# Heads of 64 features: high and low parts stacked, two products for each score and value product

## The chip, the cores and the metric

The kernel runs on one core of one Trainium2 chip. The metric is the device time of one launch in microseconds, as the median of three runs. TensorE multiplies matrices into PSUM banks of 128 x 512 numbers; VectorE, ScalarE and GpSimd work on tiles of 128 partitions; SyncE issues the DMA transfers of the weights.

## The reference

A sequence of 512 tokens with 1024 features goes through two layers of a first block (hybrid mixer, cross attention to a memory, convolutional feed-forward) and two layers of a second block. The change lies in two of the sublayers.

The mixer of the first block has two attention branches with 8 query heads and 2 key heads of 64 features each. Branch a looks at a band of 128 positions to either side, with a learned sink; branch b looks at all positions:

```
s = einsum('bnqkgd,bnskd->bnkgqs', qb, kw) / sqrt(64);  s = where(valid, s, -inf)      # branch a
p = softmax(concat([s, sink]))[..., :-1];  o = einsum('bnkgqs,bnskd->bnqkgd', p, vw)
s = einsum('bqkgd,bskd->bkgqs', qblk, k) / sqrt(64);  p = softmax(s);  o = einsum('bkgqs,bskd->bqkgd', p, v)   # branch b
```

A third branch is a gated product over positions. Each branch goes through its own weights, times a sigmoid gate of the input, and the sum through one more product. The first layer of the second block has an indexer: 16 query heads of 64 features against one key, `relu(q k)` weighted and summed over heads, of which the 256 largest per query choose the keys of another attention.

## The kernel before, in words

All products are made to float32 precision from float32r pieces: every operand is split in a high part (a rounded copy, by ScalarE) and a low part (what is left, by VectorE), and `mm3` (lines 129 to 133) issues three products for each: high by high, high by low, low by high. They run over weight units of 128 x 1024 numbers, brought by DMA and split by `W` (lines 146 and 150).

For 64 features `heads_ab` makes the queries of 4 head pairs c and the keys, turns them by TensorE transposes into feature-major tiles of 128 partitions (`to_fm`, L611), in which one head takes partitions 0 to 63 and the other 64 to 127, and splits them. A score product then contracts over 64 partitions, `r = slice(64 * half, 64 * half + 64)`. Scores of one head and one tile of 128 queries go to one of two PSUM banks (tile `pss`); a maximum (L797 in branch b, L759 with the mask in a), an exp with its sum (L800, L763) and a scaling by the reciprocal (L805, L772) make the four tiles of P, which lie in the tiles `v` for the first head of a pair and `w` for the second. `pt_av` (from L656) transposes P (L665, tile `pt`, two banks), splits it (L166 and L167, tile `t`), and multiplies by the values. The values of a pair lie side by side with 64 zero columns between them, so that both heads, one after the other, add into the two halves of one PSUM bank (tile `po`, there is one), which is split at the end of the pair. The indexer does its scores likewise in `score`, with one bank more, and ScalarE's relu frees the bank.

The program's order is not that of the code: a scheduler sets each engine's queue from its own estimate of the times, and where an attention chain has to wait, TensorE gets products of what comes next in the code. These are the products of the tile `mm`: the projections of the next branch, the gates and the branch weights (`branch`). `branch` of the gated part follows branch a, that of a and of b follow branch b, and the last needs the result of b. Three banks hold `mm` tiles, so the products of branch b's weights can't run far ahead of its attention.

Of the kernel before, what the change touches and what calls it, by code (L numbers as in the profile page):

```python
# [49 lines left out]
class Kernel:  # L50
# [65 lines left out]
    @contextmanager  # L116
    def behind(self, *marks):
        """what is issued inside follows the marked instructions on their engines."""
        with ExitStack() as es:
            for m in marks:  # L120
                es.enter_context(self.tc.issue_after(m))
            yield

    def mark(self):
        """the last instruction issued."""
        return self.nc.cur_bb.bb.instructions[-1]

# [7 lines left out]
    def W(self, ap, kc, tag=None):  # L135
        """weight unit [128, kc*w] in high and low parts; returns block k -> (high, low) [128, w]."""
# [22 lines left out]
    def split(self, role, src, n=512, scale=None):  # L159
        """src (PSUM or SBUF, f32), by row times scale -> (high, low) f32r tiles."""  # L160
# [9 lines left out]
    def lin(self, units, kc, xs, post, n=512, head=0, tail=0, mid=None, tags=(), spare=False, late=None):  # L170
        """feature-major product; unit = [128, kc*w], w/128 output chunks of kc blocks. The first head chunks
        take the two token halves one after the other; the last tail chunks do so as a group, with mid between.
        tags: where the last units' weights go; spare: two score banks are free after the head.
        late: (n, marks): the weights from unit n on are taken behind the marks."""
# [60 lines left out]
    def tok(self, units, xs, post, tiles=4, w=256):  # L235
        """token-major product; units split the contraction; psum pair tiles [128, 2, w]."""
# [13 lines left out]
    def tok_head(self, items, xs):  # L250
        """the first products (blocks, post, w) together, token half by token half; token-major, but the first."""
# [29 lines left out]
    def rstd(self, v, n):  # L281
        """v ** -0.5 on a small tile: a few by power on GpSimd and one Newton step, more from the exponent's half
        by Newton's iteration."""
# [35 lines left out]
    def sq_add(self, st, src, c, first=False):  # L319
        """src ** 2 joins the sum of squares (first: begins it for tokens c)."""  # L320
# [24 lines left out]
    def ln_chunk(self, st, xs, m, c):  # L345
        """centred chunk m joins the sums of values and squares."""
# [9 lines left out]
    def ln_pilot(self, st, x, c):  # L356
        """the mean of the first chunk, about which all statistics are taken."""
# [7 lines left out]
    def ln_stats(self, st, c, eps):  # L365
        """-> PSUM bank with 1/std and mean/std of the 256 tokens c, on all partitions."""
# [21 lines left out]
    def pipe(self, n, stages, strict=True):  # L388
        """stages of one instruction each over n items, in step: on every engine the oldest item first."""
# [8 lines left out]
    def ln_apply(self, bc, xs, g, b, c, post, own=2):  # L398
        """normalises the 256 tokens c; every own-th mean off on GpSimd (own 1: every second gain there too);
        post: what follows, a function of k per instruction."""  # L400
# [31 lines left out]
    def xsplit(self, out, src, c):  # L432
        """high and low parts of src(k) [128, tokens c] into the k-th pair of out, in two steps."""
# [33 lines left out]
    def last(self, units, kc, xs, resid, norm, tail=4, head=0, tags=(), sums=1, late=None):  # L467
        """a sublayer's last product, its norm following by token halves: norm(half) yields after the
        statistics of each stage; the first half's sums are taken behind sums chunks more of the tail."""
# [37 lines left out]
    def resid_ln(self, st):  # L507
        """adds a product to the scaled residual, centres it and takes the statistics."""
# [23 lines left out]
    def resid_part(self, st, part):  # L532
        """the same for a product in three parts: centred about the pilot of the first two."""
# [19 lines left out]
    def norm_ln(self, st, g, b, out, nxt=None):  # L553
        """post-norm by token halves into out; nxt = gain of a second (RMS) norm on top."""
# [52 lines left out]
    def to_fm(self, role, srcs, ps=None, scale=None):  # L607
        """four token-major [128, 128] pieces -> feature-major [128, 512] (high, low)."""
# [5 lines left out]

    def rope(self, src, out, tab, p, nh, dh, blocks, half):
        """src, out [128, 2, nh*dh]; tab [128, 512] = cos | signed sin, each [4 tiles, dh];
        rotates blocks of 2*half within each head of dh."""
# [19 lines left out]
    def rope_part(self, x, tab, p, nh, dh, rot):  # L637
        """in place on the first rot dims of each head of x [128, 2, nh*dh]; tab [128, 2*4*rot]."""
# [17 lines left out]
    def pt_av(self, out, pap, nkt, qr, vap, first=True, last=True, keep=None):  # L656
        """out += v^T P^T over the key tiles; pap(qt, kt) = P piece, vap(kt) = (high, low)."""
        nc = self.nc
        for kt in range(nkt):
# [11 lines left out]
            vh, vl = vap(kt)  # L671
            self.mm3(out[:, q0 * 128:q1 * 128], vh, vl, h[:, :n], l[:, :n], first and kt == 0, last and kt == nkt - 1)

# [4 lines left out]
    def heads_ab(self, l, br, xs, tabs, mid=None):  # L678
        """projections of an attention branch: q (4 head pairs) and k feature-major, v token-major; mid runs
        after the first."""  # L680
# [56 lines left out]

    def attn_a(self, qkv, sink):
        nc = self.nc
        Q, (kh, kl), V, _ = qkv  # L740
        nsink = self.sm(8)
        nc.vector.tensor_scalar(nsink, sink, -1.0, None, op0=ALU.mult)
        out = []
# [1048 lines left out]
```

## Time and profile before

| | |
|---|---|
| runs | 3522.07 us median (3520.36 to 3522.11) |
| profiled execution, span from first to last instruction | 3519.9 us |
| TensorE products | 19440, busy 98% of the span |
| VectorE, ScalarE, GpSimd | busy 60%, 43%, 11% |
| granted TensorE clock, mean | 0.991 of full speed |

A profiled execution gives its span; its own time on the device's clock isn't told, and the timed runs lie 0.5 to 2.2 us above the span. A product is shown from its issue to its modelled end, so products overlap: the distance of their starts says what one costs, not its duration. Lines are those of the kernel before.

### The profile page before, as it was taken

The numbers are of one execution on the slowest core, as the hardware profiler recorded it, in microseconds if no ns is written. First come the engines' busy times: TensorE is split into PE (matmuls) and PEld (weight loads), VectorE is DVE, ScalarE is ACT, GpSimd is POOL, SyncE is SP. The second block draws the span as 40 slices with busy tenths as digits, with TensorE's granted clock in tenths as the row PEclk, the third lists the DMA queues.
The fourth block names the chain that finished last, engine by engine and source line by source line (L and its number), as shares of the span: only waits on it lengthen the run. The fifth ranks groups of instructions, "written<-read, shape, count | busy, mean of one in ns | idle before, by whom it ended". The sixth has DMA issues, their size and how long they took to land.

```text
span 3519.9 us, 49472 instructions
## 1 busy us (share of the span) xinstructions
PE 3442.7 (98%) x19440; PEld 2977.4 (85%) x19440; DVE 2122.4 (60%) x3874; ACT 1498.4 (43%) x2786; POOL 385.1 (11%) x588
## 2 busy tenths in 40 slices
PE   9999999999999999999999998999999998999999
PEld 8897798888898877988888788889888887988887
DVE  5576587655665765775557578565333698664333
ACT  3444355433434444553334446353222576442222
POOL 0000012000000000120001243000000286110000
PEclk9999999999999999999999998999999999999999
DMA  4221231333322212313333122222333322223333
GB/s 143 72 64 58 63 124 60 96 98 96 97 90 68 72 49 80 113 61 108 96 96 88 48 81 83 78 91 83 96 97 95 101 73 84 78 67 92 100 96 96
DMA packets 87929, 302.40 MB, mean 86 GB/s; under 512 B 10000, under 2 KB 10768, under 8 KB 87696
## 3 DMA queue, kind: packets, MB, share of 16 engines
q1 hardware_dynamic: 87696, 299.24, 27.9%
q8 instruction: 153, 2.51, 0.3%
q14 instruction: 80, 0.66, 0.1%
HBM read 297.10 MB, written 2.10 MB: 85 GB/s over the span
## 4 chain that ended last, share of the span: by engine, by line
PE 75%; issue 12%; DVE 7%; POOL 2%; ACT 2%; DMA 2%; DVEq 0%; POOLq 0%; ACTq 0%
PE mm L131 20%; PE mm L132 20%; PE mm L133 20%; PE pss L131 2%; PE pss L133 2%; PE pss L132 2%; PE pt L665 2%; PE mm L195 1%; PE po L132 1%; PE po L131 1%; PE po L133 1%; DVE wl L150 1%; PE po L195 1%; DVE pss L1414 1%; PE mm L198 1%
## 5 line engine op out<-in xcount | busy, mean ns | idle before, releaser
L146 ACT CAST wh<-wraw 128x1024 fp32r<-128x1024 f32 (+2 forms) x496 | 514.0, 1039 | 953.3 <-PE mm L132 475.5
L150 DVE TENSOR_TENSOR wl<-wraw,wh 128x1024 fp32r<-128x1024 f32 (+2 forms) x487 | 599.2, 1232 | 509.8 <-ACT wh L146 504.1
L131 PE MATMUL mm<-xh,wh 128*128 128x512 f32 (+1 forms) x2152 | 821.5, 382 | 8.2 <-ACT xh L437 6.0
L132 PE MATMUL mm<-xl,wh 128*128 128x512 f32 (+1 forms) x2152 | 822.8, 382 | 1.2 <-DVE xl L440 1.1
L133 PE MATMUL mm<-xh,wl 128*128 128x512 f32 (+1 forms) x2152 | 820.8, 381 | 0.0
L131 PEld LDWEIGHTS mm<-xh,wh 128*128 128x128 f32 x2152 | 405.5, 189 | 86.6 <-ACT xh L437 6.4
L132 PEld LDWEIGHTS mm<-xl,wh 128*128 128x128 f32 x2152 | 405.6, 188 | 82.4 <-issue 5.5
L133 PEld LDWEIGHTS mm<-xh,wl 128*128 128x128 f32 x2152 | 405.5, 188 | 80.1 <-issue 5.6
L131 PE MATMUL mm<-wh,xh 128*128 128x256 f32 x768 | 220.2, 287 | 0.0
L133 PE MATMUL mm<-wh,xl 128*128 128x256 f32 x768 | 219.1, 285 | 0.0
L132 PE MATMUL mm<-wl,xh 128*128 128x256 f32 x768 | 219.0, 285 | 0.0
L131 PE MATMUL mm<-p,wh 128*128 128x512 f32 (+1 forms) x556 | 202.1, 371 | 6.3 <-DVE x L524 4.3
L133 PE MATMUL mm<-p,wl 128*128 128x512 f32 (+1 forms) x556 | 205.1, 369 | 0.0
L132 PE MATMUL mm<-p,wh 128*128 128x512 f32 (+1 forms) x556 | 204.0, 367 | 0.0
L376 POOL TENSOR_TENSOR s<-s 128x2 f32<-128x2 f32 x14 | 7.0, 502 | 1576.8 <-ACT s L373 1576.8
L131 PE MATMUL mm<-o,wh 128*128 128x512 f32 (+1 forms) x456 | 170.2, 373 | 0.0
L132 PE MATMUL mm<-o,wh 128*128 128x512 f32 (+1 forms) x456 | 169.4, 371 | 0.0
L133 PE MATMUL mm<-o,wl 128*128 128x512 f32 (+1 forms) x456 | 169.2, 371 | 0.0
L1123 DVE TENSOR_TENSOR x<-x,mm 128x512 f32<-128x512 f32 (+1 forms) x102 | 57.0, 565 | 164.7 <-PE mm L133 164.6
L131 PEld LDWEIGHTS mm<-wh,xh 128*128 128x128 f32 x768 | 146.8, 191 | 4.6 <-issue 3.9
L133 PEld LDWEIGHTS mm<-wh,xl 128*128 128x128 f32 x768 | 146.9, 191 | 4.2 <-issue 3.9
L132 PEld LDWEIGHTS mm<-wl,xh 128*128 128x128 f32 x768 | 146.9, 191 | 3.5 <-issue 2.6
(636 smaller groups left out, 7166.8 us busy)
## 6 DMA issues: line engine op xcount, KB each, us to landing
wraw<-fup SPq DMA_DIRECT2D x88, 512.0 KB, 3.5
wraw<-gup SPq DMA_DIRECT2D x88, 512.0 KB, 3.6
wraw<-wg SPq DMA_DIRECT2D x48, 512.0 KB, 3.5
wraw<-wt SPq DMA_DIRECT2D x32, 512.0 KB, 3.5
wraw<-fdn SPq DMA_DIRECT2D x32, 512.0 KB, 3.5
wraw<-gdn SPq DMA_DIRECT2D x32, 512.0 KB, 3.5
wraw<-wbr SPq DMA_DIRECT2D x24, 512.0 KB, 3.5
wraw<-wab SPq DMA_DIRECT2D x20, 512.0 KB, 3.5
```

Of the source, the lines that this page charges most:

```text
L131: mm(out, lh, rh, start=first, stop=False, skip_group_check=True)
L132: mm(out, lh, rl, start=False, stop=False, skip_group_check=True)
L133: mm(out, ll, rh, start=False, stop=last, skip_group_check=True)
L146: nc.scalar.copy(h[i][:, :e], raw[:, i * e:(i + 1) * e])
L150: eng.tensor_tensor(l[i][:, :e], raw[:, i * e:(i + 1) * e], h[i][:, :e], op=ALU.subtract)
L195: self.nc.tensor.matmul(out, w[:, c], xs[k][0][:, t], start=first and k == 0 and w is h, stop=False, skip_group_check=True)
L198: self.nc.tensor.matmul(out, h[:, c], xs[k][1][:, t], start=False, stop=k == kc - 1, skip_group_check=True)
L376: g.tensor_tensor(t, m, m, op=ALU.mult)
L665: nc.tensor.transpose(ps[:, i * 128:(i + 1) * 128], pap(qt, kt), self.ident)
L1123: self.nc.vector.tensor_add(x, x, ps)
L1414: nc.vector.scalar_tensor_tensor(acc[:, s:], a[:, :S - s], w(s), acc[:, s:], op0=ALU.mult, op1=ALU.add)
```

## The change

`to_stack` replaces `to_fm` for queries of 64 features. For each head of a pair it makes a tile of its own, with the head's high part on one half of the partitions and its low part on the other, by a copy of 64 partitions and a subtraction of 64 partitions, whose result goes to the other half. `to_twice` writes the keys of each key head twice, on both halves, as a high and a low tile. Two products over 128 partitions (`mm2`) then hold all four terms: stacked query by high key, stacked query by low key. The values get their low columns where the zeros were: a tile of 128 columns holds a head's high and low part. Two products with the high and low part of P give the two halves in the two halves of the partitions of a PSUM bank, and `join` adds them: a ScalarE copy of 64 partitions to the place of the head, and a VectorE addition. The bank `po` is thus taken and freed once a head, not once a pair; the split follows from SBUF. The indexer's queries are stacked in the same way; its key was on both halves before. Attention with 128 features keeps `mm3`.

```diff
+    def to_stack(self, role, srcs):
+        nc = self.nc
+        ps = self.pst()
+        for i, a in enumerate(srcs):
+            nc.tensor.transpose(ps[:, i * 128:(i + 1) * 128], a, self.ident)
+        out = []
+        for r, q in ((slice(0, 64), slice(64, 128)), (slice(64, 128), slice(0, 64))):
+            t = self.T(role, F32R)
+            nc.scalar.copy(t[r], ps[r])
+            nc.vector.tensor_sub(t[q], ps[r], t[r])
+            out.append(t)
+        return out
+    def to_twice(self, role, srcs):
+        nc = self.nc
+        ps = self.pst()
+        for i, a in enumerate(srcs):
+            nc.tensor.transpose(ps[:, i * 128:(i + 1) * 128], a, self.ident)
+        out = []
+        halves = slice(0, 64), slice(64, 128)
+        for r in halves:
+            h, l = self.T(role, F32R), self.T(role, F32R)
+            for q in halves:
+                nc.scalar.copy(h[q], ps[r])
+                nc.vector.tensor_sub(l[q], ps[r], h[q])
+            out.append((h, l))
+        return out
+    def mm2(self, out, q, kh, kl):
+        mm = self.nc.tensor.matmul
+        mm(out, q, kh, start=True, stop=False, skip_group_check=True)
+        mm(out, q, kl, start=False, stop=True, skip_group_check=True)
...
-            vh, vl = vap(kt)
-            self.mm3(out[:, q0 * 128:q1 * 128], vh, vl, h[:, :n], l[:, :n], first and kt == 0, last and kt == nkt - 1)
+            v, o = vap(kt), out[:, q0 * 128:q1 * 128]
+            if isinstance(v, tuple):
+                self.mm3(o, *v, h[:, :n], l[:, :n], first and kt == 0, last and kt == nkt - 1)
+                continue
+            nc.tensor.matmul(o, v, h[:, :n], start=first and kt == 0, stop=False, skip_group_check=True)
+            nc.tensor.matmul(o, v, l[:, :n], start=False, stop=last and kt == nkt - 1, skip_group_check=True)
+    def join(self, out, o, half):
+        r, q = (slice(64 * i, 64 * i + 64) for i in (half, 1 - half))
+        self.nc.scalar.copy(out[r], o[q])
+        self.nc.vector.tensor_add(out[r], out[r], o[r])
...
-            vh, vl = self.T("r", F32R, [128, 2, 3, 64]), self.T("r", F32R, [128, 2, 3, 64])
-            z = self.ident.rearrange("p (t c) -> p t c", t=2)
-            nc.vector.tensor_scalar(vh[:, :, 1], z, 0.0, None, op0=ALU.mult)
-            nc.vector.tensor_scalar(vl[:, :, 1], z, 0.0, None, op0=ALU.mult)
+            v = self.T("r", F32R, [128, 2, 4, 64])
             src = ps[:, :, 128:256].rearrange("p t (h c) -> p t h c", h=2)
-            nc.scalar.copy(vh[:, :, 0::2], src)
-            nc.vector.tensor_sub(vl[:, :, 0::2], src, vh[:, :, 0::2])
-            V[p] = (vh.rearrange("p t a c -> p t (a c)"), vl.rearrange("p t a c -> p t (a c)"))
+            nc.scalar.copy(v[:, :, 0::3], src)
+            nc.vector.tensor_sub(v[:, :, 1:3], src, v[:, :, 0::3])
+            V[p] = v.rearrange("p t a c -> p t (a c)")
...
-        Q = [self.to_fm("q", [qt[c // 2, t // 2][:, t % 2, (c % 2) * 128:(c % 2 + 1) * 128] for t in range(4)]) for c in range(4)]
-        Kt = self.to_fm("r", [kt[t // 2][:, t % 2, :] for t in range(4)])
+        Q = [self.to_stack("q", [qt[c // 2, t // 2][:, t % 2, (c % 2) * 128:(c % 2 + 1) * 128] for t in range(4)]) for c in range(4)]
+        Kt = self.to_twice("r", [kt[t // 2][:, t % 2, :] for t in range(4)])
...
     def attn_b(self, qkv):
         nc = self.nc
-        Q, (kh, kl), V, rq = qkv
+        Q, Kt, V, rq = qkv
         out = []
         for c in range(4):
-            o = self.po()
+            both = self.T("w")
             for half in range(2):
-                r = slice(64 * half, 64 * half + 64)
+                o = self.po()
+                kh, kl = Kt[half]
                 P = []
                 nm, sm = self.sm(4), self.sm(4)
                 for qt in range(4):
                     ps = self.pss()
-                    self.mm3(ps, Q[c][0][r, qt * 128:(qt + 1) * 128], Q[c][1][r, qt * 128:(qt + 1) * 128],
-                             kh[r, :], kl[r, :], True, True)
+                    self.mm2(ps, Q[c][half][:, qt * 128:(qt + 1) * 128], kh, kl)
                     i = ((c // 2) * 2 + qt // 2) * 8 + (qt % 2) * 4 + (c % 2) * 2 + half
                     nc.vector.tensor_reduce(nm[:, qt:qt + 1], ps, axis=AX.X, op=ALU.max, negate=True)
                     nc.vector.tensor_tensor(nm[:, qt:qt + 1], nm[:, qt:qt + 1], rq[:, i:i + 1], op=ALU.mult)
...
                 nc.vector.reciprocal(sm, sm)
                 for qt in range(4):
                     nc.vector.tensor_scalar(P[qt], P[qt], sm[:, qt:qt + 1], None, op0=ALU.mult)
-                vap = lambda kt: tuple(a[:, kt % 2, 64 * half:64 * half + 128] for a in V[kt // 2])
-                self.pt_av(o, lambda qt, kt: P[qt][:, kt * 128:(kt + 1) * 128], 4, lambda kt: (0, 4), vap,
-                           half == 0, half == 1)
-            out.append(self.split("p", o))
+                vap = lambda kt: V[kt // 2][:, kt % 2, 128 * half:128 * half + 128]
+                self.pt_av(o, lambda qt, kt: P[qt][:, kt * 128:(kt + 1) * 128], 4, lambda kt: (0, 4), vap)
+                self.join(both, o, half)
+            out.append(self.split("p", both))
...
-            r = slice(64 * (h % 2), 64 * (h % 2) + 64)
             s = slice(qt * 128, (qt + 1) * 128)
             ps = self.po() if qt == 2 else self.pss()
-            self.mm3(ps[:, :n], Q[0][r, s], Q[1][r, s], ikh[r, :n], ikl[r, :n], True, True)
+            self.mm2(ps[:, :n], Q[h % 2][:, s], ikh[:, :n], ikl[:, :n])
...
-                Q = self.to_fm("op"[u // 2], [it[u][t // 2][:, t % 2, c * 128:(c + 1) * 128] for t in range(4)])
+                Q = self.to_stack("op"[u // 2], [it[u][t // 2][:, t % 2, c * 128:(c + 1) * 128] for t in range(4)])
```

`attn_a` is changed as `attn_b`. The scheduler then sets another order. On TensorE, in branch b of the first layer, in the last head pair (P in `w` is of the pair's second head, P in `v` of the first; `pss` are scores, `pt` transposes, `po` value products, `mm` products of other work), before:

```order
L132 MATMUL po<-t,r 128x512
L133 MATMUL po<-t,r 128x512
L665 MATMUL pt<-ident,w 128x128 x6
L131 MATMUL pss<-r,q 128x512
L132 MATMUL pss<-r,q 128x512
L133 MATMUL pss<-r,q 128x512
L131 MATMUL pss<-r,q 128x512
L132 MATMUL pss<-r,q 128x512
L133 MATMUL pss<-r,q 128x512
L132 MATMUL mm<-xl,wh 128x512
L133 MATMUL mm<-xh,wl 128x512
L131 MATMUL mm<-o,wh 128x512
```

And now, at the same place (the last `v` tiles are that pair's first head):

```order
L714 MATMUL po<-t,r 128x512
L703 MATMUL pt<-ident,v 128x128 x4
L713 MATMUL po<-t,r 128x512
L714 MATMUL po<-t,r 128x512
L713 MATMUL po<-t,r 128x512
L714 MATMUL po<-t,r 128x512
L649 MATMUL pss<-r,q 128x512
L650 MATMUL pss<-r,q 128x512
L649 MATMUL pss<-r,q 128x512
L650 MATMUL pss<-r,q 128x512
L703 MATMUL pt<-ident,w 128x128 x8
L713 MATMUL po<-t,r 128x512
```

Before, twelve and more `mm` products follow a group of scores; now the scores of the next tiles, the transposes and the value products stand next to one another.

On ScalarE at this place (`t` is a part of P transposed, `p` a part of the result, `wh` a weight's high part, `f` a gate), before:

```order
L800 ACTIVATE v,s<-pss,s 128x512 x2
L166 CAST t<-pt 128x512 x2
L800 ACTIVATE v,s<-pss,s 128x512 x2
L146 CAST wh<-wraw 128x1024
L883 ACTIVATE f<-mm,pv 128x512
L166 CAST t<-pt 128x512 x2
L800 ACTIVATE w,s<-pss,s 128x512 x2
L166 CAST p<-po 128x512
L166 CAST t<-pt 128x512 x2
```

And now:

```order
L719 COPY w<-po 64x512
L166 CAST t<-pt 128x512
L166 CAST p<-w 128x512
L166 CAST t<-pt 128x512 x3
L719 COPY w<-po 64x512
L847 ACTIVATE w,s<-pss,s 128x512 x4
L166 CAST t<-pt 128x512
L847 ACTIVATE v,s<-pss,s 128x512 x2
L166 CAST t<-pt 128x512 x2
L847 ACTIVATE v,s<-pss,s 128x512 x2
```

Copies of the join (`w<-po`) stand ahead of the exps of the next head (L847) and of the cast of the pair's result (`p<-w`), once a head; weight casts and gates are gone from the stretch.

## Rows read from the trace of the kernel before

**Rows 1.** the page: busy shares of engines, then the chain that ended last

```profile
PE 3442.7 (98%) x19440; PEld 2977.4 (85%) x19440; DVE 2122.4 (60%) x3874; ACT 1498.4 (43%) x2786; POOL 385.1 (11%) x588
...
PE 75%; issue 12%; DVE 7%; POOL 2%; ACT 2%; DMA 2%; DVEq 0%; POOLq 0%; ACTq 0%
```

**Rows 2.** stretches: length, then PE, PEld, DVE, ACT, POOL busy, clock, DMA

```profile
181.00:250.00 69.00, 69.00 (x488) 63.58 (x487) 51.41 (x150) 29.85 (x67) 0.00 (x0) 1.00 0.20 62
...
310.00:360.00 50.00, 50.00 (x235) 38.57 (x233) 34.26 (x67) 23.99 (x46) 0.00 (x0) 1.00 0.18 53
1990.00:2060.00 70.00, 70.00 (x433) 55.03 (x432) 39.66 (x58) 35.94 (x88) 14.87 (x22) 1.00 0.15 46
```

**Rows 3.** TensorE's timeline in branch b: start, duration, instruction

```profile
370.41 0.40 PE L132 MATMUL mm<-xl,wh 128*128 128x512 f32 x1
370.74 0.49 PE L131 MATMUL pss<-r,q 64*128 64x512 f32 x1
371.07 0.39 PE L132 MATMUL pss<-r,q 64*128 64x512 f32 x1
371.31 0.39 PE L133 MATMUL pss<-r,q 64*128 64x512 f32 x1
371.63 0.50 PE L133 MATMUL mm<-xh,wl 128*128 128x512 f32 x1
371.96 0.40 PE L131 MATMUL mm<-xh,wh 128*128 128x512 f32 x1
372.20 0.39 PE L132 MATMUL mm<-xl,wh 128*128 128x512 f32 x1
372.43 0.40 PE L133 MATMUL mm<-xh,wl 128*128 128x512 f32 x1
```

**Rows 4.** lines by form, branch b: count, busy us, mean ns, idle before

```profile
L797 DVE TENSOR_REDUCE s<-pss 128x1 f32<-128x512 f32 x32 | 21.8, 687 | 4.7 <-PE pss L133 4.5
L167 DVE TENSOR_TENSOR t<-pt,t 128x512 fp32r<-128x512 f32 x30 | 20.4, 685 | 16.5 <-ACT t L166 16.5
...
L805 DVE TENSOR_SCALAR w<-w,s 128x512 f32<-128x512 f32 x16 | 6.7, 482 | 0.1
...
L798 DVE TENSOR_TENSOR s<-s 128x1 f32<-128x1 f32 x32 | 4.6, 154 | 0.2
...
L166 ACT CAST t<-pt 128x512 fp32r<-128x512 f32 x31 | 17.1, 590 | 20.6 <-PE pt L665 20.6
...
L800 ACT ACTIVATE v<-pss,s 128x512 f32<-128x512 f32 x16 | 12.4, 777 | 20.7 <-DVE s L798 20.7
...
L800 ACT ACTIVATION_READ_ACCUMULATOR w<-pss,s 128x1 f32 x16 | 3.1, 194 | 0.0
```

**Rows 5.** timeline of branch b's last transposes and its end

```profile
396.22 0.60 PE L665 MATMUL pt<-ident,w 128*128 128x128 f32 x4
396.57 0.48 PE L132 MATMUL po<-t,r 128*128 128x512 f32 x1
...
403.33 0.51 PE L131 MATMUL mm<-p,wh 128*128 128x512 f32 x1 [0.68 <-ACT p L166]
```

**Rows 6.** lines by form of VectorE, branch a

```profile
L167 DVE TENSOR_TENSOR t<-pt,t 128x384 fp32r<-128x384 f32 x16 | 8.9, 554 | 6.2 <-ACT t L166 6.2
L167 DVE TENSOR_TENSOR t<-pt,t 128x256 fp32r<-128x256 f32 x16 | 6.7, 420 | 3.8 <-ACT t L166 3.7
L761 DVE TENSOR_SCALAR s<-s 128x1 f32<-128x1 f32 x32 | 6.0, 208 | 0.1
...
L759 DVE CUSTOM_DVE_ANT_0 w<-pss,mask 128x384 f32<-128x384 f32 x8 | 4.4, 552 | 0.8 <-PE pss L133 0.7
...
L772 DVE TENSOR_SCALAR w<-w,s 128x384 f32<-128x384 f32 x8 | 3.0, 415 | 0.0
```

**Rows 7.** a stretch of few products: busy times and clock

```profile
2150.00:2160.00 10.00, 7.21 (x18) 3.88 (x19) 6.58 (x11) 8.16 (x17) 2.78 (x8) 0.52 0.38 122
```

**Rows 8.** TensorE's timeline in that stretch

```profile
2155.68 0.80 PE L131 MATMUL mm<-v,wh 128*128 128x512 f32 x1 [0.55 <-ACT v L166]
```

More of the change, by code (lines that the diff above doesn't have):

```diff
@@ L739, in attn_a @@
         nc = self.nc
-        Q, (kh, kl), V, _ = qkv
+        Q, Kt, V, _ = qkv
         nsink = self.sm(8)
@@ L754, in attn_a @@
                     ps = self.pss()
-                    self.mm3(ps[:, :n], Q[c][0][r, qt * 128:(qt + 1) * 128], Q[c][1][r, qt * 128:(qt + 1) * 128],
-                             kh[r, k0 * 128:k1 * 128], kl[r, k0 * 128:k1 * 128], True, True)
+                    self.mm2(ps[:, :n], Q[c][half][:, qt * 128:(qt + 1) * 128], kh[:, k0 * 128:k1 * 128],
+                             kl[:, k0 * 128:k1 * 128])
                     pt = self.T("vw"[half])
@@ L776, in pap @@
                     return P[qt][:, o0:o0 + 128]
-                vap = lambda kt: tuple(a[:, kt % 2, 64 * half:64 * half + 128] for a in V[kt // 2])
-                self.pt_av(o, pap, 4, lambda kt: (max(0, kt - 1), min(4, kt + 2)), vap, half == 0, half == 1)
-            out.append(self.split("o", o))
+                vap = lambda kt: V[kt // 2][:, kt % 2, 128 * half:128 * half + 128]
+                self.pt_av(o, pap, 4, lambda kt: (max(0, kt - 1), min(4, kt + 2)), vap)
+                self.join(both, o, half)
+            out.append(self.split("o", both))
         return out
@@ L783, in attn_b @@
         nc = self.nc
-        Q, (kh, kl), V, rq = qkv
+        Q, Kt, V, rq = qkv
         out = []
         for c in range(4):
-            o = self.po()
+            both = self.T("w")
             for half in range(2):
-                r = slice(64 * half, 64 * half + 64)
+                o = self.po()
+                kh, kl = Kt[half]
                 P = []
@@ L805, in attn_b @@
                     nc.vector.tensor_scalar(P[qt], P[qt], sm[:, qt:qt + 1], None, op0=ALU.mult)
-                vap = lambda kt: tuple(a[:, kt % 2, 64 * half:64 * half + 128] for a in V[kt // 2])
-                self.pt_av(o, lambda qt, kt: P[qt][:, kt * 128:(kt + 1) * 128], 4, lambda kt: (0, 4), vap,
-                           half == 0, half == 1)
-            out.append(self.split("p", o))
+                vap = lambda kt: V[kt // 2][:, kt % 2, 128 * half:128 * half + 128]
+                self.pt_av(o, lambda qt, kt: P[qt][:, kt * 128:(kt + 1) * 128], 4, lambda kt: (0, 4), vap)
+                self.join(both, o, half)
+            out.append(self.split("p", both))
         return out
```

## The prediction

> **What bounds the kernel now.** I read the busy shares first: TensorE is busy 98% of a span of 3519.9 us, VectorE 60%, ScalarE 43% [rows 1]. The chain that ended last confirms it: 75% of it is TensorE's. The timed runs lie at 3520.36 to 3522.11, so about 2.2 us of the median stand outside the profiled span; I sum against the span and add 2.2.
>
> The change touches three stages, so I then took the stretches. In both attention branches (181 to 250, 310 to 360) and in the indexer (1990 to 2060) TensorE is busy in every microsecond, VectorE in 57 to 75% [rows 2]. So there a product taken away should come off the end one for one, as long as something else is ready to run. The reader should keep the second half of that sentence: nothing idles today because products of the gates and branches (the tiles mm, "filler" below) fill TensorE while one head's chain of reduce, exp, transpose and cast runs on VectorE and ScalarE.
>
> **What it removes.** Per layer, branch a has 8 heads of 1280 score columns and as many value columns, branch b 8 heads of 2048 of each; the indexer has 16 heads of 1152 score columns. One of three products goes in each: 2 x (20,480 + 32,768) + 18,432 = 124,928 columns. Neighbouring 512-column products start 0.23 us apart (372.20 and 372.43; 371.07 and 371.31 for two with 64 rows) [rows 3]; with 0.227 that is 0.443 ns a column and 55.4 us. Branch a's narrower products are in this by columns.
>
> There is a second saving, which the diff does not show. Where a 64-row score product stands beside 128-row products, starts are 0.33 us apart instead of 0.23: 370.41 to .74, .74 to 371.07, 371.31 to .63, .63 to .96 [rows 3]. That is four times 0.10, 0.41 us for each run of 64-row products. In the issue order I count 124 such runs (84 in the two mixers, 40 in the indexer): 50.8 us. The new scores contract over 128 rows, so the neighbours match. Sum so far -106.2 us. If the gap belongs to the scores and not to their rows, 0 of the 50.8 comes; I take all of it, since both edges of a run pay on both sides.
>
> The Trainium skill speaks against the change here: TensorEngine Tiling (Array Packing), Theoretical Speedup, gives up to twofold for contractions of 64 or less, because tiles of 64 rows can work at once. By that the three 64-row products would cost as much as one and a half, and the scores' part of the sum would be +13.8 us instead of -27.7. The trace does not bear it out: 64-row products follow each other at 0.24 and no faster, and no two heads' products alternate in it.
>
> **What it adds.** Splits of q into 64-partition pieces, of k twice over, a join of the two value halves: I count 60 more ScalarE copies and 44 more VectorE operations in the mixers net of the four zero fills per branch, 8 and 8 more in the indexer. A 64-partition one is not in the trace; by its neighbours it lies between 0.3 (half the work) and 0.69 us, and I take 0.59 and 0.69, the 512-column rows [rows 4]. The shift to other partitions is unpriced; between no cost and doubled for the 120 pieces, all of it beside TensorE. Where those engines have room this costs nothing; the indexer keeps its filler in the new order (some 6 to 20 products between scores), and VectorE has about 30 us of 70 free there [rows 2]. I book 0 for it.
>
> **What is late next.** The chain of one head does not get shorter, while TensorE's share of it does. In the new issue order the filler is used up early: about 24 us of it stand before the second head of branch b, and from the middle of the second head pair only 13, 9 and 0 filler products remain for the rest. The old order still has 12 to 17 between score groups up to the last. So TensorE's work in the last stretch of b is: first cycle 32 products of 0.227, 32 transposes of 0.088 (four in 0.35, 396.22 to 396.57 [rows 5]) and 13 fillers, 13.0 us; second cycle with 9 fillers 12.1; last part 4.1.
>
> I walked one cycle (last value product of a pair's first head to the same of the next pair) through the queues with the durations in [rows 4, 5], links of 0.03 us, and back-to-back steps as the rows show (exp 0.77, reduce and subtraction 0.60, scale 0.42). 0: product ends. ScalarE's queue has the join's copy first, then two exps: 0.62, 1.40, 2.17. Each exp frees a score bank; two products take 0.62; the fourth tile's reduce ends at 3.58. Its exps and sum end at 5.42, reciprocal and four scalings at 7.35, transposes 7.75. The next head's two reduces and multiplies run to 8.84, its exps to 10.28, and only then come the casts: subtractions end at 9.53, 11.58, 12.32 and, behind two more exps, 15.2. Scaling of the next head ends at 17.6, the join at 18.4, its four subtractions at 19.3, 20.5, 21.3, 22.4, the last product at 22.9. So 22.9 us a cycle, of which VectorE's queue alone is 18.5 (8 reduces, 8 multiplies, 8 scalings, 8 subtractions, 2 joins, a split, 2 reciprocals). TensorE idles 9.9, 10.8 and, in the last part (14.1 walked, less the 0.68 idle at 403.33 today [rows 5]), 9.3: 30.0 us a layer.
>
> Branch a has the same shape: 10.8 us of TensorE work with no filler in the third pair. VectorE's queue there sums to 24.8 by its rows [rows 6]: 16 subtractions, 8 masked reduces with their reads, 12 scalings, 8 small minima, 3 joins, 3 full-width operations and the start of the next projection's rotation. 14.0 us idle. Two layers: 88.0.
>
> One price is not sure: in [rows 7] the clock fell to 0.52 of 2.4 GHz, that is, mostly 1.2, in 10 us with 18 products, and such products then take 0.80 us instead of 0.39 [rows 8]. The first 7 us of each cycle hold six products. Four product pairs a cycle on the path, up to 0.5 us longer each, 2 us; four cycles a layer, two layers, 16 at most, 0 at least; I take half for a mixed clock, 8.
>
> Sum: -55.4 - 50.8 + 88.0 + 8.0 = -10.2; 3519.9 - 10.2 + 2.2 = **3512 us**. Most of the saving is given back. Bounds: idle half as long as walked (the chain overlaps better), -62; idle 30% longer with the clock down throughout, +24.
>
> **Rivals.** (1) TensorE stays the bound: for it speaks its 100% in [rows 2]; against it the order without filler. 3522 - 106 = 3416 at the far end, 3465 with half the idle time: chance 0.17. (2) Slower: the score chain of branch b becomes the bound from the second pair on. It decides once idle exceeds 53 us a layer against 44 and 4 in my sum: cycles of 27 us in b, with the join's copy holding up the exps in every pair, the same share more in a, and the clock down throughout make 62 and give 3540. For it: VectorE and ScalarE already wait for each other in the tail of today [rows 5]; against it, every walked link is short. 0.27. The Trainium skill says of the clock (TensorE: Matmul & The Clock Gate, What's actually happening) that the throttled state is the default and activity releases it; [rows 7] agrees. (3) The 0.10 us gaps stay, because transposes keep interrupting the products: 3522 - 55 + 88 = 3555 less idle time that the gaps then cover, some 3545: 0.06. (4) The forecast, idle between 30 and 50 us a layer: 0.50, range 3490 to 3530.
>
> **Numbers.** 0.2% (7 us) is what a measurement can tell. Of the forecast's 0.50 I put 0.28 on faster by more than that, 0.16 within, 0.06 slower. With rival 1 faster is 0.45; within 0.17 with 0.01 from rival 2; slower 0.38. The range 3465 to 3548 leaves out the far ends of rivals 1 and 2.
>
> **What would show it.** The score products get 128 rows and lose the 0.33 us steps; their columns fall by a third: if not, the first two terms fail. TensorE drops to about 60% busy somewhere in the last 60 us of b's scores in each mixer, waiting for the t casts and subtractions and the exps, and less so in a; the indexer shortens by some 20 us at full busy share. If TensorE stays at 100% in the mixers rival 1 holds; if the mixers get longer than today by over 10 us each, rival 2.

## The result, and the profile after

The changed kernel takes 3544.43 us (median of 4 runs, 3543.43 to 3549.45) against 3521.64 us of the kernel before: 1.0067 times, 95% interval 1.0053 to 1.0081. It is slower, where the forecast said 3512.

The page after, busy shares and the chain that ended last, answers to [rows 1]:

```profile
PE 3396.8 (96%) x19136; PEld 2953.1 (83%) x19136; DVE 2168.1 (61%) x3926; ACT 1538.4 (43%) x2854; POOL 386.6 (11%) x588
...
PE 83%; DVE 7%; ACT 3%; POOL 3%; issue 2%; DMA 1%; ACTq 0%; POOLq 0%; DVEq 0%
```

TensorE was busy 98% of a shorter span and is now busy 96%: 46 us less busy time in a span that is 22 us longer. Where the time went is read from the starts of instructions that both kernels have, behind the stages of the change. First three of the kernel before (ScalarE's timeline; a cast in the sublayer behind the first mixer, a copy ahead of the indexer's sublayer, a square behind it):

```profile
656.36 0.62 ACT L166 CAST p<-w 128x512 fp32r<-128x512 f32 x1 [2.79 <-DVE w L593]
...
1792.34 0.57 ACT L363 COPY c<-pt 128x512 f32<-128x512 f32 x1
...
2250.45 0.42 ACT L328 ACTIVATE f<-x 128x256 f32<-128x256 f32 x1 [2.46 <-DVE x L1123]
```

and the same three after:

```profile
674.00 0.62 ACT L166 CAST p<-w 128x512 fp32r<-128x512 f32 x1 [2.79 <-DVE w L593]
...
1833.38 0.58 ACT L363 COPY c<-pt 128x512 f32<-128x512 f32 x1
...
2272.05 0.42 ACT L328 ACTIVATE f<-x 128x256 f32<-128x256 f32 x1 [2.46 <-DVE x L1170]
```

They start 17.6, 41.0 and 21.6 us later. So the stretch up to behind the first mixer lost 17.6 us, the stretch from there to the indexer's sublayer, which holds the second mixer, another 23.4, and the indexer's sublayer gained 19.4. Columns and steps were taken out of the mixers as well, so there more than these was paid back.

The stretches after, columns as in [rows 2]: branch a's later heads, branch b, the end of branch b, the indexer.

```profile
180.00:250.00 70.00, 60.41 (x397) 53.52 (x396) 54.61 (x170) 35.71 (x89) 0.00 (x0) 0.93 0.13 39
320.00:425.00 105.00, 83.09 (x340) 57.15 (x339) 64.50 (x129) 48.38 (x96) 0.00 (x0) 0.90 0.08 26
400.00:420.00 20.00, 12.63 (x43) 7.80 (x41) 9.09 (x18) 7.90 (x16) 0.00 (x0) 0.74 0.00 0
2010.00:2060.00 50.00, 49.97 (x397) 48.88 (x397) 36.10 (x51) 33.97 (x69) 15.50 (x29) 1.00 0.24 75
```

For branch b [rows 2] stop at 360 us; up to its end the kernel before shows:

```profile
310.00:405.00 95.00, 93.89 (x440) 71.83 (x439) 58.01 (x113) 44.32 (x84) 0.00 (x0) 1.00 0.15 45
```

In the indexer TensorE stays busy, as it was. In branch a's stretch it now idles 9.6 of 70 us, in branch b's 21.9 of 105 (1.1 of 95 before), and the granted clock is 0.93, 0.90 and at the end 0.74, where it was 1.00. What TensorE waited for in branch b, from 320 to 425 us (total us, times, longest):

```profile
PE pss L649 <- ACT w L847: 7.5, 5, 2.2
PE mm L131 <- ACT p L166: 3.5, 2, 2.0
PE po L713 <- ACT t L166: 3.4, 7, 0.6
```

The largest wait is of score products for exps that write the tiles w, which belong to the second heads of pairs. The steps of 0.33 us beside score products are gone, though; TensorE's timeline, answering to [rows 3]:

```profile
281.30 0.39 PE L133 MATMUL mm<-o,wl 128*128 128x512 f32 x1
281.53 0.39 PE L649 MATMUL pss<-r,q 128*128 128x512 f32 x1
281.76 0.39 PE L650 MATMUL pss<-r,q 128*128 128x512 f32 x1
281.98 0.39 PE L131 MATMUL mm<-o,wh 128*128 128x512 f32 x1
```

Filler and scores follow each other at 0.22 to 0.23 us.

The reason for that wait shows in the first pair of branch b. VectorE's timeline after: the second head's maxima.

```profile
289.21 0.69 DVE L844 TENSOR_REDUCE s<-pss 128x1 f32<-128x512 f32 x1 [0.80 <-PE pss L650]
...
291.48 0.69 DVE L844 TENSOR_REDUCE s<-pss 128x1 f32<-128x512 f32 x1 [0.37 <-PE pss L650]
292.20 0.16 DVE L845 TENSOR_TENSOR s<-s 128x1 f32<-128x1 f32 x1
```

By 292.4 us the first two tiles of the second head can be exponentiated. ScalarE's timeline after, same head:

```profile
299.64 1.08 ACT L166 CAST t<-pt 128x512 fp32r<-128x512 f32 x2 [5.97 <-PE pt L703]
...
303.06 1.06 ACT L146 CAST wh<-wraw 128x1024 fp32r<-128x1024 f32 x1 [0.80 <-PE mm L132]
306.46 0.58 ACT L719 COPY w<-po 64x512 f32<-64x512 f32 x1 [2.34 <-PE po L714]
307.07 0.78 ACT L847 ACTIVATE w<-pss,s 128x512 f32<-128x512 f32 x1
...
307.84 0.77 ACT L847 ACTIVATE w<-pss,s 128x512 f32<-128x512 f32 x1
```

The exps start at 307.07, 14.7 us later. ScalarE was free meanwhile (it idled 5.97 us before 299.64). In its queue these exps stand behind the join's copy of the first head (L719), which waits for that head's last value product. In the kernel before the second head's exps ran among the first head's casts:

```profile
283.89 0.78 ACT L800 ACTIVATE w<-pss,s 128x512 f32<-128x512 f32 x1 [2.28 <-DVE s L798]
...
284.66 0.58 ACT L166 CAST t<-pt 128x512 fp32r<-128x512 f32 x1
285.13 0.79 ACT L800 ACTIVATE w<-pss,s 128x512 f32<-128x512 f32 x1
...
286.84 0.60 ACT L166 CAST t<-pt 128x512 fp32r<-128x512 f32 x1
291.22 0.78 ACT L800 ACTIVATE w<-pss,s 128x512 f32<-128x512 f32 x1 [3.78 <-DVE s L798]
...
293.00 0.78 ACT L800 ACTIVATE w<-pss,s 128x512 f32<-128x512 f32 x1 [0.92 <-DVE s L798]
```

So the heads of a pair, which overlapped, now follow one another. The distance from the first pair's first head's last value product to the second head's (starts of the products po<-t,r) says what it costs: 25.8 us in branch a and 25.9 in b, against 13.7 and 16.5 before. TensorE does not idle there. It spends filler: 96 and 86 of the products mm lie between these two, where 36 and 34 lay before, and the last five heads of branch b find 4, 9, 0, 9 and 0.

### The profile page after: what moved, and what is told of

It reads as the page before. It is cut to its first block, busy times and chain, and to the rows that moved or that the text cites. A ratio compares the mean times of both kernels' runs of the same rounds, so it can differ in the third digit from the quotient of the medians.

```text
span 3542.1 us, 49037 instructions
## 1 busy us (share of the span) xinstructions
PE 3396.8 (96%) x19136; PEld 2953.1 (83%) x19136; DVE 2168.1 (61%) x3926; ACT 1538.4 (43%) x2854; POOL 386.6 (11%) x588
## 4 chain that ended last, share of the span: by engine, by line
PE 83%; DVE 7%; ACT 3%; POOL 3%; issue 2%; DMA 1%; ACTq 0%; POOLq 0%; DVEq 0%
PE mm L131 23%; PE mm L132 23%; PE mm L133 23%; PE pt L703 2%; PE mm L195 1%; PE pss L133 1%; PE pss L132 1%; PE pss L131 1%; DVE wl L150 1%; PE pss L649 1%; PE pss L650 1%; PE mm L198 1%; PE po L195 1%; PE po L714 1%; POOL v L1454 1%
## 5 line engine op out<-in xcount | busy, mean ns | idle before, releaser
L131 PEld LDWEIGHTS mm<-xh,wh 128*128 128x128 f32 x2152 | 405.9, 189 | 83.6 <-ACT xh L437 6.4
```

What stands on the lines that cost most here:

```text
L131: mm(out, lh, rh, start=first, stop=False, skip_group_check=True)
```

## Experiments

Times are medians beside runs of the kernel before on the same chip (3520.4 to 3521.4); ratios have 95% intervals. "Late" and "early" say where the first head's join stands.

**1. The indexer alone** (all lines of the mixers as before).

```diff
-            self.mm3(ps[:, :n], Q[0][r, s], Q[1][r, s], ikh[r, :n], ikl[r, :n], True, True)
+            self.mm2(ps[:, :n], Q[h % 2][:, s], ikh[:, :n], ikl[:, :n])
...
-                Q = self.to_fm("op"[u // 2], [it[u][t // 2][:, t % 2, c * 128:(c + 1) * 128] for t in range(4)])
+                Q = self.to_stack("op"[u // 2], [it[u][t // 2][:, t % 2, c * 128:(c + 1) * 128] for t in range(4)])
```

> Only the indexer changed, both mixers as before. The changed kernel's indexer ended about 19 us earlier than that of before by the times of like instructions. If that gain is its own, the whole is 3502 to 3505 us. If it came from work that the longer mixers had already done for it, the gain goes with them and the time is 3515 to 3522.

Measured 3499.63 us, 0.9939 [0.9925, 0.9954]: 21.8 us gained, a little below both ranges. The indexer's part of the change is good by itself, and did not take its gain from the mixers.

**2. The step beside 64-row products**, in the indexer of the kernel before.

```diff
-        ikh, ikl = self.to_fm("r", [ikt[t // 2][:, t % 2] for t in range(4)])
+        ik = []
+        for r, q in ((slice(0, 64), slice(64, 128)), (slice(64, 128), slice(0, 64))):
+            kh, kl = self.T("r", F32R), self.T("r", F32R)
+            nc.scalar.copy(kh[r], ps[r])
+            nc.vector.tensor_sub(kl[r], ps[r], kh[r])
+            for k in (kh, kl):
+                nc.vector.tensor_scalar(k[q], ps[q], 0.0, None, op0=ALU.mult)
+            ik.append((kh, kl))
...
-            self.mm3(ps[:, :n], Q[0][r, s], Q[1][r, s], ikh[r, :n], ikl[r, :n], True, True)
+            self.mm3(ps[:, :n], Q[0][:, s], Q[1][:, s], ikh[:, :n], ikl[:, :n], True, True)
```

> The kernel before, but the indexer's key is laid out twice, each time with zeros for the other head, so that its three score products contract over 128 rows; as many products and columns as before. If the step of 0.10 us comes from 64 rows standing beside 128 rows, 40 runs of scores x 0.41 us go: 3505 to 3508 us. If it belongs to score products as such, or to what stands between them: 3520 to 3523.

Measured 3509.43 us, 0.9966 [0.9953, 0.9979]: 12.0 us by the medians, 15.1 by the profiled spans (the execution profiled was the fastest of five), with as many columns as before. The 40 runs were priced at 16.4, so the median lies just behind its range; what held the rest back was not looked into. Its scores among 256-column filler, TensorE's timeline:

```profile
1998.38 0.40 PE L131 MATMUL pss<-r,o 128*128 128x512 f32 x1
1998.61 0.40 PE L132 MATMUL pss<-r,o 128*128 128x512 f32 x1
1998.84 0.39 PE L133 MATMUL pss<-r,o 128*128 128x512 f32 x1
1999.07 0.28 PE L132 MATMUL mm<-wl,xh 128*128 128x256 f32 x1
```

0.23 us from score to score and from the last to the filler; the step is gone. It belongs to the rows. The Trainium skill (TensorEngine Tiling (Array Packing), Key Properties) says that a change of tiling mode drains the engine. The page does not say that a 64-row product among 128-row ones is such a change; the trace would fit it, with two start distances longer by 0.10 us at each edge of a run.

**3. The join late.** The same for branch b.

```diff
-            both = self.T("w")
             for half in range(2):
...
                 vap = lambda kt: V[kt // 2][:, kt % 2, 128 * half:128 * half + 128]
+                if half:
+                    both = self.T("w")
+                    self.join(both, first, 0)
+                first = o
                 self.pt_av(o, pap, 4, lambda kt: (max(0, kt - 1), min(4, kt + 2)), vap)
-                self.join(both, o, half)
+                if half:
+                    self.join(both, o, half)
```

> The changed kernel, but the join of a pair's first head, and the tile it writes, stand in the program behind the scores and exps of the second head. Same operations, counts, banks and buffers. Theory A: the loss of the mixers comes from the exps of every second head standing behind that join (its tile takes its place in the buffers w ahead of them), so that the two heads of a pair run one after the other; then the mixers lose their 18 and 22 us and gain some: 3440 to 3495 us. Theory B: the chain of one head with its added splits and copies and the single bank for value products sets the time, filler being short in any order: 3530 to 3550 us.

Measured 3463.04 us, 0.9836 [0.9821, 0.985]: 81 us faster than the changed kernel with the same operations. ScalarE's timeline in the first pair of branch b:

```profile
278.04 0.78 ACT L850 ACTIVATE w<-pss,s 128x512 f32<-128x512 f32 x1 [0.93 <-DVE s L848]
...
279.30 0.78 ACT L850 ACTIVATE w<-pss,s 128x512 f32<-128x512 f32 x1 [0.39 <-DVE s L848]
...
280.06 1.06 ACT L166 CAST t<-pt 128x512 fp32r<-128x512 f32 x2
284.28 0.78 ACT L850 ACTIVATE w<-pss,s 128x512 f32<-128x512 f32 x1 [3.15 <-DVE s L848]
...
286.10 0.78 ACT L850 ACTIVATE w<-pss,s 128x512 f32<-128x512 f32 x1 [0.95 <-DVE s L848]
...
295.21 0.58 ACT L719 COPY w<-po 64x512 f32<-64x512 f32 x1
```

The second head's exps run from 278 to 286 us, ahead of the first head's copy at 295.21, and the distance of the first two heads' ends is 13.6 us in branch a and 16.7 in b again. Theory A holds. What remains lies in the last heads of both branches; the stretches of b:

```profile
300.00:340.00 40.00, 40.00 (x197) 33.18 (x196) 29.73 (x59) 22.87 (x43) 0.00 (x0) 1.00 0.19 66
340.00:385.00 45.00, 38.59 (x164) 27.16 (x163) 31.35 (x64) 24.33 (x49) 0.00 (x0) 0.90 0.04 13
```

**4. and 5. A third product in the mixers**, with the late join and with the early one (the results take one term twice).

```diff
         mm(out, q, kh, start=True, stop=False, skip_group_check=True)
+        if thrice:
+            mm(out, q, kl, start=False, stop=False, skip_group_check=True)
         mm(out, q, kl, start=False, stop=True, skip_group_check=True)
...
+            nc.tensor.matmul(o, v, l[:, :n], start=False, stop=False, skip_group_check=True)
             nc.tensor.matmul(o, v, l[:, :n], start=False, stop=last and kt == nkt - 1, skip_group_check=True)
```

> The same, and in the mixers the second of the two products is issued twice for scores and values, so that 106,496 columns of 128 rows come back (the results take one term twice). If TensorE bounds the mixers again once the join stands late, all of it is paid: 47 us over the kernel with the late join. If the chain on VectorE and ScalarE bounds them, 0 to 15 us over it.

> The changed kernel with its early join, and in the mixers the second of the two products issued twice for scores and values (106,496 columns of 128 rows more, 47 us of TensorE; the results take one term twice). Theory A: the heads of a pair run one after the other, TensorE waits for them, and the columns that the change removed are worth little there: 0 to 18 us over the changed kernel's 3544, 3544 to 3562. If TensorE's work were the bound: 3591.

Measured 3479.94 us with the late join (0.9883 [0.9866, 0.9899]), 16.9 over experiment 3, between the two forecasts; 3555.97 with the early one (1.0094 [1.0079, 1.0109]), 11.5 over the changed kernel, as theory A had it. So of the 47.2 us of columns that the mixers lost, 11.5 showed in the changed kernel; the rest did not come off the end.

**6. and 7. More filler for branch b's last heads**, with the late join and with the early one, by the same edit in `branch`:

```diff
+        def gate(k, wg, tag="f"):
+            pg = self.mm()
+            for q in range(NK):
+                self.mm3(pg, *wg(q), xs[q][0], xs[q][1], q == 0, q == NK - 1)
+            t = self.T(tag)
+            nc.scalar.activation(t, pg, AF.Tanh, scale=0.5, bias=self.col(f"bg{l}", 8 * n + k))
+            return t
+        early = [gate(k, self.W(d[f"wg{l}"][8 * n + k], NK), tag) for k, tag in enumerate(ahead)]
         for k in range(NK):
...
-        self.branch(l, 1, ob, xs, mrg)
+        self.branch(l, 1, ob, xs, mrg, "fffqqq")
```

> The kernel with the late join (3463), and the gates of the last branch are issued ahead of its products with branch b's result, six of eight, three of them into buffers that the queries of branch b leave. Same operations. In the issue order 72 more products of other work then stand between the last heads of branch b in each layer (42, 40, 15, 0 where 16, 0, 9, 0 stood). If what is left of the loss is TensorE running out of other work in b's last heads, 12 to 15 us a layer come back: 3433 to 3442 us. If these heads are bound otherwise, or the last weights come late by the buffers, 3455 to 3470.

> The changed kernel with its early join and the gates ahead in the same way: more other work, but the heads of a pair still one after the other. The order puts the added products between the first heads, and leaves 9, 0, 9, 0 between the last ones. If lack of other work by itself made the change slow, 3500 to 3515 us; if it is the place of the join, the last heads stay as they are: 3530 to 3545.

Measured 3444.5 us late (0.978 [0.9764, 0.9796]) and 3518.13 early (0.9992 [0.9983, 1.0001]). Late, 18.5 us came back, less than the 24 hoped for. Early, 26 came back, outside both forecasts: besides filling gaps between the first heads, the order also put 50 filler products between the two heads of the second pair, where 4 stood, which I had not counted. More filler helps either way; with the pairs in series it only makes up what the change lost.

**8. and 9. The values alone**, early and late join; scores and indexer as before.

```diff
-                    self.mm2(ps, Q[c][half][:, qt * 128:(qt + 1) * 128], kh, kl)
+                    self.mm3(ps, Q[c][0][r, qt * 128:(qt + 1) * 128], Q[c][1][r, qt * 128:(qt + 1) * 128],
+                             kh[r, :], kl[r, :], True, True)
```

> Only the values of the mixers changed (two products and the join, early as in the changed kernel); scores of 64 rows with three products, indexer as before. If the join's place carries the loss, this is slower than before although 53,248 columns, 23.6 us, are gone: 3545 to 3585 us. If the scores' part of the change (more splits, its shorter products) carried it, this gains: 3498 to 3515.

> Only the values of the mixers changed, with the late join; scores of 64 rows with three products and the indexer as before. With the early join this took 3597. If the place of the join alone made that loss, most of the 23.6 us of removed columns now shows: 3500 to 3515 us. If the two-product values cost by themselves (bank taken per head, more operations), 3520 to 3550.

Measured 3596.83 us early (1.0214 [1.0199, 1.0229]), worse than forecast, and 3527.12 late (1.0015 [1.0006, 1.0025]), a miss for the first theory. The join's place costs 70 us here too. But even late, 53,248 columns fewer brought nothing. Why the early one came out behind its range is open.

**10. Gates ahead in the kernel before.**

> The kernel before with the gates ahead alone. In its trace TensorE waits only some 2 us in the last heads of branch b of a layer, so there is little for them to fill: 3516 to 3523 us. If the gates ahead are worth something by themselves (weights, banks), below 3512.

Measured 3519.18 us, 0.9995 [0.9985, 1.0004]: the gates ahead are worth nothing where nothing idles.

**11. and 12. Two faster versions**: all eight gates ahead (`"fffqqqqq"`), and with them other buffers for branch b's projections (tag is f for branch b, v else):

```diff
-                qt[u, p] = self.T("w", shape=[128, 2, 256])
+                qt[u, p] = self.T("p" if isb else "w", shape=[128, 2, 256])
...
-            kt[p] = self.T("w", shape=[128, 2, 128])
+            kt[p] = self.T("p" if isb else "w", shape=[128, 2, 128])
...
-        a, b = self.T("v"), self.T("v")
+        a, b = self.T(tag), self.T(tag)
```

> Late join and all eight gates of the last branch ahead, five of them in the buffers of branch b's queries. The order leaves 46 and 17 products in the last two heads of branch b, where six gates left 15 and 0. With six gates TensorE still lost some 7 us a layer there: 3430 to 3438 us if that goes, 3444 or more if the eighth gate's buffers hold up the weights after it.

> The same, and branch b's rotated queries and keys and the work tiles of their rotation lie in buffers that branch a's attention does not use (p and f for w and v), so that branch b's projections need not wait for branch a's last heads. The order puts 53 and 85 products of other work between branch a's last heads where 8 and 24 stood, and 28, 9, 0 between branch b's. If TensorE's loss of some 9 us a layer in branch a's last heads comes from these buffers, it goes, and part of it is lost again in branch b: 3420 to 3436 us. If not, 3436 to 3450.

Measured 3440.38 us (0.9771 [0.9754, 0.9787]) and 3437.49 (0.9758 [0.9743, 0.9772]). Both beat both kernels; their intervals overlap. Number 11 lies between its two ranges, number 12 in the range of the case that went against it. The stretches of 11, branch a's last heads and the end of branch b:

```profile
195.00:220.00 25.00, 20.85 (x137) 19.09 (x136) 19.67 (x58) 13.04 (x34) 0.00 (x0) 0.86 0.06 22
360.00:390.00 30.00, 30.00 (x150) 24.96 (x149) 19.84 (x38) 17.00 (x31) 0.00 (x0) 1.00 0.21 71
390.00:400.00 10.00, 7.73 (x32) 5.47 (x31) 2.93 (x5) 2.37 (x4) 0.00 (x0) 0.86 0.00 0
```

and of 12:

```profile
195.00:240.00 45.00, 44.61 (x318) 41.98 (x318) 36.71 (x107) 21.92 (x49) 0.00 (x0) 1.00 0.23 71
360.00:400.00 40.00, 35.62 (x165) 27.50 (x164) 28.07 (x53) 21.77 (x41) 0.00 (x0) 0.96 0.11 31
```

In 11 TensorE idles 4.2 us and its clock drops in branch a's last heads; in 12 it idles 0.4 at the full clock, since branch b's projections can run there. At the end of b 4.4 us of idle time stand in 12 against 2.3 in 11, since b's filler is now spent earlier.

**13. and 14. What the values lose, and whether TensorE bounds again.** Number 9 and number 11 with additions already shown (eight gates; third product, one term twice).

> Only the values of the mixers changed, with the late join, as in the run that took 3527, and all eight gates of the last branch ahead. If the removed value columns showed nothing there because TensorE ran out of other work in branch b's last heads (it lost some 17 us a layer), they show now: 3495 to 3506 us. If the two-product values lengthen the heads by their own operations and bank, wherever other work stands: 3515 to 3530.

> The kernel with late join and eight gates ahead (3440), and in the mixers the second of the two products issued twice for scores and values (47 us of TensorE; the results take one term twice). If TensorE bounds this kernel throughout, what is saved against the kernel before is the step beside 64-row products and the indexer's columns, 50.8 and 8.2 us: 3463 to 3475. If the chains of the heads bound it still, 3440 to 3455.

Number 13 took 3521.92 us, 1.0003 [0.9993, 1.0012]. Its time is in the range of the second theory, but most of it not by its mechanism. The end of branch b:

```profile
360.00:415.00 55.00, 55.00 (x241) 39.71 (x240) 30.70 (x58) 28.19 (x51) 0.00 (x0) 1.00 0.19 57
415.00:430.00 15.00, 11.99 (x50) 8.72 (x49) 5.99 (x11) 4.12 (x7) 0.00 (x0) 0.89 0.01 4
```

TensorE is busy up to the last head. In this order the 64-row scores of the mixers stand in 112 separate runs, not 84, and the start distances around them exceed the usual ones by 51.2 us in sum, not 36.4. Of the 23.6 us of columns 14.8 went into that. Some 10 us are left; the idle end, 3.0 us a layer in this stretch, is 6 of them, and the others I did not separate, so a part of the second theory may hold.

Number 14 took 3465.8 us, 0.9846 [0.9832, 0.9861], as forecast for a kernel that TensorE bounds:

```profile
195.00:240.00 45.00, 45.00 (x352) 44.11 (x351) 37.70 (x101) 22.51 (x50) 0.00 (x0) 1.00 0.22 66
360.00:400.00 40.00, 40.00 (x200) 33.31 (x199) 21.61 (x40) 19.82 (x38) 0.00 (x0) 1.00 0.17 53
```

No idle time is left in either stretch, and 54.6 us stand between it and the kernel before, where the steps beside 64 rows and the indexer's columns sum to 59.0. From here to number 11, taking 47.2 us of columns out gives 25.4.

## Why the prediction was wrong, step by step

- **What it removes** held in its two terms. Experiments 2 and 14 confirm the 0.10 us steps of [rows 3] and that 128 rows end them. The columns are there as well; how much of them shows depends on the filler (11.5, 16.9 and 25.4 of 47.2 us in three kernels). The pair of figures beside them, +13.8 against -27.7, took half of all columns for the scores; they are 71,680 of 124,928, so that it would be +15.9 against -31.8. Nothing in the sum hangs on it.
- **The indexer**: the forecast's two terms are 24.6 us (8.2 of columns, 16.4 of steps); the trace shows 19.4, the run alone 21.8. Booking no loss there was nearly right.
- **The step that failed** is what is late next: the idle term, "30.0 us a layer" in b and 14.0 in a, with 8 us for the clock, 96 us in all. The mixers gave back 17.6 + 23.4 + 83.6 = 124.6 us (83.6 being what was taken out of them: 47.2 of columns, 36.4 of steps). The sum priced the heads that I walked and put nothing on the others. The walk itself came near in b: its last part was put at 14.1 us and took 14.3 (402.5 to 416.8, last value products), its cycles at 22.9 and took 25.3 and 25.0, slow products included. In a the third pair was put at 24.8 us and took 18.9 (204.0 to 222.9).
  An estimate from start distances (what they exceed the usual ones by, less the 0.5 us a head that busy stretches show too) puts some 87 us on the stretches walked, in both layers, against the 96 booked. Some 30 us lie in heads that the sum put at nothing, 23 of them in branch a and 7 in b's second pair; the last 7 or so are not placed. So it was in part luck that the walked stretches came near their price: a's third pair was put too long, the clock too short.
  Behind them stands what the walk left out. I had the join's copy ahead of the second head's exps in the order, and walked it for the last pairs only. In the first pairs, where filler hides it, I took the heads to cost nothing. There it holds the second head back by 9 to 12 us, and TensorE spends filler on it that the old order kept for the end. Experiment 3 moves that one join and gets 81 us. Not all of the loss is the join's: by the same estimate experiment 3 still loses some 8 us a layer in branch a.
- **The clock** was the second short term. It lies within the 124.6 us. Products that ran at the lower of its two levels (those shown with over 1.5 times the usual duration) stood further apart by 23 us in sum, or by 30 if distances above twice the usual are counted in full, against 8 booked; nearly half of it in the second layer's branch b. Answering to [rows 8], in the last head:

```profile
404.62 0.50 PE L649 MATMUL pss<-r,q 128*128 128x512 f32 x1 [1.57 <-ACT w L847]
...
405.71 0.40 PE L650 MATMUL pss<-r,q 128*128 128x512 f32 x1
408.85 1.94 PE L703 MATMUL pt<-ident,w 128*128 128x128 f32 x8 [2.74 <-DVE w L852]
411.31 0.80 PE L713 MATMUL po<-t,r 128*128 128x512 f32 x1 [0.52 <-ACT t L166]
```

A value product takes 0.80 us after waits of 2.74 and 0.52 us. [rows 7] and [rows 8] had shown this price; taking half of it was a guess with no row behind it.
- **The rivals.** The outcome is rival 2, which named the join's copy ahead of the exps, asked for over 53 us a layer (59 and 65 came, the clock in them) and said 3540. Its sum of 62 a layer is nearer than its terms: it asked for cycles of 27 us and the clock down throughout, and the cycles took 25.3 and 25.0 in the first layer, with a granted clock of 0.90 over the stretch. I gave it less than the forecast since "every walked link is short"; the links are, but a queue's order is not a link. Rival 1's 3465 is near where the same operations stand with the join late (3463), though TensorE does not bound that kernel throughout.

That the exps are queued behind the copy because the tile `both` takes its place in the buffers w ahead of the second head's P is read from the two issue orders and from experiment 3; no run took the buffers away alone. Moving the join also lets the scheduler set the rest of the order anew, so the 81 us are those of the new order as a whole; the place of the exps is what the traces show changed in it. Open too is what keeps 24 us between 3440 and the 3416 of the first sum; the idle ends in the stretches of 11 are some 6.5 us a layer of it, before their lower clock.

## What to carry to other kernels

Filler is a stock. Before removing work from the bounding engine, count the filler that each head will use at the head's new length, from the first head on, and not only what is left at the end. A new temporary that shares a ring of buffers with a later stage may put that stage behind its own producer (the ring's part in it is argued here, not shown alone). Write it in program order behind the stage that must not wait: here the same operations stood 81 us apart. The Trainium skill (Perfetto Trace Analysis, Optimization Strategy) says that a gap that keeps returning on the engine that should be saturated can come from missing room for the next tile; here the trace agrees for branch a's last heads, where other buffers took the idle time from 4.2 us to 0.4 (experiments 11 and 12). In the first pairs, where the second heads came 9 to 12 us late, there is no gap to see, since filler covers it.

## What the runs showed of the hardware

The step beside 64-row products is 0.09 to 0.11 us on each of two start distances at either edge of a run, for 256, 384 and 512 columns, and goes when the operand is padded with zeros to 128 rows (experiment 2). So it counts runs, not products: an order that scatters the same 64-row products over 112 runs instead of 84 cost 14.8 us (experiment 13).

Operations on 64 partitions, which the prediction had no row for, cost what those on 128 do: in the changed kernel a copy of 64 x 512 numbers takes 0.58 us and a subtraction or addition 0.69, also where the result goes to the other 64 partitions.
